# Nine modulation pieces moved from the state-space groups into the first group's projections of a hybrid diffusion layer

## The chip, the cores and the metric

The kernel runs on one core of one Trainium2 chip. The metric is device time in microseconds (us): the median over runs of the whole kernel. TensorE (PE) multiplies, with its weight loads shown apart (PEld); VectorE (DVE), ScalarE (ACT) and GpSimd (POOL) do the element-wise work; SyncE (SP) issues nearly all of the transfers.

## The reference, cut to what matters

One layer of a diffusion backbone over 512 latent tokens and 256 context tokens, model width 1024, in float32:

```
mod = silu(c) @ w_mod + b_mod                      # six vectors of 1024: sh1 sc1 gt1 sh2 sc2 gt2
h_lat, h_ctx = modulated RMSNorm of x and of ctx   # needs sh1, sc1 only
p = h @ w_in                                       # z | x, B, C | dt | q k v | gates
x, B, C = silu(conv3(p[x, B, C]))                  # three taps along the tokens
y = bidirectional chunked state-space scan of (x, B, C, dt), 4 groups of 8 heads, 4 chunks of 128 tokens
a = windowed attention with rotary embedding, context keys and a sink
out = (g_ssd * (norm(y*silu(z)) @ w_o_ssd) + g_att * (a @ w_o_att)) @ w_out
x = x + gt1 * out;  x = x + gt2 * convffn(modulate(x, sh2, sc2));  final RMSNorm
```

The last four of the six modulation vectors (gt1, sh2, sc2, gt2: 4 x 1024 numbers) are what the moved pieces work on. They are first used after the state-space part.

## The kernel before

Every float32 product is made of three reduced-precision products: a weight tile `wraw` is rounded to `whi` on ScalarE (line 149), the rest `wlo` is formed on VectorE (line 150), and TensorE multiplies `whi` with the high and low part of the activations and `wlo` with the high part (lines 197, 198 and 200 in `gemm`). A weight tile is 128 x 1024 float32, 512 KB.

**Loads.** `load_raw` (line 145) issues a tile's transfer on SP's queue into one of three `wraw` buffers. `whi` and `wlo` have two buffers each. `run(prog)` walks a list of steps, each with the weight tiles that it needs; before a step's instructions are recorded, the loads up to one tile beyond that step are recorded, in the order of the list. A buffer is taken again when the last reader of its old tile is done: for a projection's tile that is the split on lines 149 and 150, for a modulation tile the second operation of its piece.

**The stretch around the change.** After the attention comes the state-space part (its list is built at lines 1523 to 1545). `proj_steps(g)` gives six projections for group g. In this document those of the first group are called b (B), c (C) and x0 to x3. Each multiplies a tile with the latent tokens (24 matmuls of 512 columns) and, except c, with the context tokens (24 of 256 columns). `conv_silu` then makes the convolution: one ScalarE operation (line 1267), two on VectorE (1268, 1269), a tanh on ScalarE (1275) and a last VectorE operation (1276), for the latent tokens and then for the context. The result is transposed on TensorE within the next projection (line 1295) and copied out by ScalarE. `ssd_steps(g)` then does the scan of group g, chunk by chunk, woven with a `z` projection and the projections of group g+1. After x3 the first of these, called z15 here, is a gate projection with the latent tokens alone.

**The modulation pieces.** `m_step(i)` (line 569) is a piece of the product of silu(c) with the modulation matrix. It needs one 512 KB tile `wm2`, which goes through the same three `wraw` buffers but is not split: two VectorE operations on 128 x 512 multiply its halves with two columns of `csil` and add to `tm`, of which there is one buffer (lines 581 and 583). Four pieces make one column group; after the fourth, four transposes on TensorE (line 591) and two short VectorE operations (lines 593, 594) put the sums into `mod2`. There are 32 pieces. Pieces 0 to 8 (m0 to m8 here) lie in the state-space groups 0 to 2, three in each; the others come later.

**What sets the order.** The steps' list sets the order in which the code records instructions, and a scheduler then orders each engine's instructions and assigns the buffers. `tc.issue_after(i)` keeps the operations recorded within it from standing ahead of instruction i.

Of the kernel before, what the change touches and what calls it, by code (L numbers as in the profile page):

```python
# [1 line left out]

# [1 line left out]

# [9 lines left out]
ALU = mybir.AluOpType  # L14
# [30 lines left out]
def tile_hybrid_layer(  # L45
# [33 lines left out]
    V, S, G, T = nc.vector, nc.scalar, nc.gpsimd, nc.tensor  # L79
# [28 lines left out]
    def accb():  # L108
        return bank("acc")

    def misb():
        return bank("mis")
# [3 lines left out]
    def tmp(tag):  # L116
        return tpool.tile([P, 512], F32, tag=tag, name=tag, bufs=TMP[tag])
# [73 lines left out]
    def gemm(targets, w, nk=KT, m=P, k0=0, first=True, last=True, ks=None):  # L191
        hi, lo = w
        for k in range(nk) if ks is None else ks:
            wh, wl = hi[:, k * m : (k + 1) * m], lo[:, k * m : (k + 1) * m]
            a, b = first and k == 0, last and k == nk - 1
            for ps, xh, xl in targets:
                T.matmul(ps, wh, xh[:, k0 + k, :], start=a, stop=False)  # L197
                T.matmul(ps, wh, xl[:, k0 + k, :], start=False, stop=False)  # L198
            for ps, xh, xl in targets:
                T.matmul(ps, wl, xh[:, k0 + k, :], start=False, stop=b)  # L200
            if BETWEEN and k % 3 == 1:
                BETWEEN.pop(0)()
# [12 lines left out]
    csil = cpool.tile([P, KT, 2], F32, name="csil")  # L215
# [88 lines left out]
    with tc.tile_pool(name="spool", bufs=1) as sp:  # L304
# [131 lines left out]
        r, W, H = {}, {}, {}  # L436
# [50 lines left out]
        rows = {}  # L487
# [47 lines left out]
        for i in range(NG):  # L535
            t = tmp("tb")
# [33 lines left out]
    def m_step(i):  # L570
        cg, kk = i // 4, i % 4

        def fn(r):
            if kk == 0:
                macc[0] = tmp("tm")
            acc = macc[0]
            for u in range(2):
                k = 2 * kk + u
                sc = csil[:, k, 0:1]
                if k == 0:  # L580
                    V.tensor_scalar_mul(acc, r[:, 0:512], sc)
                else:
                    V.scalar_tensor_tensor(acc, r[:, u * 512 : u * 512 + 512], sc, acc, ALU.mult, ALU.add)
            if kk == 3 and cg > 5:
                ps = misb()
                T.matmul(ps, ones, acc, start=True, stop=True)
                V.tensor_tensor(F["g2"][cg - 6], ps, F["g2"][cg - 6], ALU.add)
            elif kk == 3:
                ps = misb()
                for c in range(4):  # L590
                    T.transpose(ps[:, c * P : (c + 1) * P], acc[:, c * P : (c + 1) * P], ident)
                z = slice(4 * cg, 4 * cg + 4)
                V.tensor_reduce(mod2[:, z], ps.rearrange("p (c q) -> p c q", c=4), axis=AX.X, op=ALU.add)
                V.tensor_tensor(mod2[:, z], mod2[:, z], vec[:, V_BMOD + 16 + 4 * cg : V_BMOD + 20 + 4 * cg], ALU.add)

        return [("m", i)], fn
# [68 lines left out]
    Q, F = {}, {}  # L665
# [600 lines left out]
    def conv_half(ps, n, base_w, base_b, i, stride, o):  # L1266
        S.activation(o[:, :n], ps[:, :n], AF.Identity, scale=hcol(base_w, stride + i), bias=hcol(base_b, i))  # L1267
        V.scalar_tensor_tensor(o[:, 1:n], ps[:, 0 : n - 1], hcol(base_w, i), o[:, 1:n], ALU.mult, ALU.add)  # L1268
        V.scalar_tensor_tensor(o[:, 0 : n - 1], ps[:, 1:n], hcol(base_w, 2 * stride + i), o[:, 0 : n - 1], ALU.mult, ALU.add)  # L1269

    def conv_silu(ps, n, i, o):
        a = tmp("ta")
        conv_half(ps, n, V_CW, V_CB, i, 24, a)
        t = tmp("tb")
        F["conv"] = S.activation(t[:, :n], a[:, :n], AF.Tanh)  # L1275
        V.scalar_tensor_tensor(o[:, :n], t[:, :n], 1.0, a[:, :n], ALU.add, ALU.mult)

    def flat(a):
        return a.rearrange("p a b -> p (a b)")
# [10 lines left out]
    def turn(n=None):  # L1290

        for t, n_, put in TURN[:n]:
            ps = misb()
            for c in range(n_):
                T.transpose(ps[:, c * P : (c + 1) * P], t[:, c * P : (c + 1) * P], ident)
            put(ps)
        del TURN[:n]

    def proj_steps(g):
        d = GR[g]  # L1300

        def b_fn(w):
            d["xs"] = bp.tile([P, 4, 512], F32, tag="xs", name="xs", bufs=2)
            d["xsc"] = bp.tile([P, 2, 512], F32, tag="xsc", name="xsc", bufs=1)
            d["Bkc"] = bp.tile([P, 2, P], F32, tag="Bkc", name="Bkc", bufs=2)
            d["Bk"] = bp.tile([P, 4, P], F32, tag="Bk", name="Bk", bufs=2)
            d["BT"] = bp.tile([P, L], F32, tag="BT", name="BT", bufs=2)
            pl, pc = accb(), accb()
            gemm([LAT(pl)], w)
            turn()  # L1310
            gemm([CTX(pc)], w)
            conv_silu(pl, L, 16 + g, d["BT"])
            BTc = tmp("tc")
            conv_silu(pc, LC, 16 + g, BTc)
            for t, n, k in ((d["BT"], 4, d["Bk"]), (BTc, 2, d["Bkc"])):
                TURN.append((t, n, lambda ps, n=n, k=k: S.copy(flat(k), ps[:, : n * P])))

        def c_fn(w):
            d["CT"] = bp.tile([P, L], F32, tag="CT", name="CT", bufs=2)
            pl = accb()  # L1320
            gemm([LAT(pl)], w)
            turn()
            conv_silu(pl, L, 20 + g, d["CT"])

        def x_fn(ct, w):
            i = 4 * g + ct
            pl, pc = accb(), accb()
            gemm([LAT(pl)], w)
            turn()
            gemm([CTX(pc)], w)  # L1330
            for pp, n, dst in ((pl, L, d["xs"]), (pc, LC, d["xsc"])):
                xl = tmp("tc")
                conv_silu(pp, n, i, xl)
                TURN.append(
                    (
                        xl,
                        n // P,
                        lambda ps, n=n, dst=dst: S.copy(
                            dst[:, :, ct * P : (ct + 1) * P], ps[:, :n].rearrange("p (a b) -> p a b", b=P)
                        ),  # L1340
                    )
                )

        r = [([("x", 16 + g)], b_fn), ([("x", 20 + g)], c_fn)]
        for ct in range(4):
            r.append(([("x", 4 * g + ct)], lambda w, ct=ct: x_fn(ct, w)))
        return r
# [173 lines left out]
        return r + [([], gate)]  # L1521

    msteps = [m_step(i) for i in range(32)]
    prog = proj_steps(0)
    for g in range(4):
        s = ssd_steps(g)
        f = fill[n2 + g : n2 + 1 + g]
        b = proj_steps(g + 1) if g < 3 else fill[n2 + 4 : n3]
        m = msteps[3 * g : 3 * g + 3] if g < 3 else []

        prog += s[0:1] + f + b[0:1] + s[1:2] + m[0:1] + b[1:2]
        for c in range(4):
            prog += s[3 * c + 2 : 3 * c + 3] + (s[3 * c + 4 : 3 * c + 5] if c < 3 else [])
            if g == 3 and c:
                prog += s[3 * c : 3 * c + 1]
            prog += b[2 + c : 3 + c]
            if c == 1:
                prog += b[6:]
            if g < 3 or c == 3:
                prog += s[3 * c + 3 : 3 * c + 4]  # L1540
            if c in (1, 2):
                prog += m[c : c + 1]
        prog += s[13:14]
    run(prog)
    bpool.close()
# [616 lines left out]
```

## Time and profile before

| | |
|---|---|
| median of 3 runs | 1232.01 us (1231.84 to 1232.99) |
| profiled execution: its time | 1232.22 us |
| profiled execution: its span | 1230.4 us |
| what lies outside the span | 1.8 us |
| modulation tiles: time to landing, median of 32 | 4.1 us |

The span runs from the first to the last instruction of one profiled execution; the views give times from its start. The first group's projections stand at 368 to 418 us. A row of the timeline has the start, the duration, the engine and line, the operation with its output and inputs, and in brackets how long the engine was idle before it and what ended that.

### The profile page before, as it was taken

Reading aid. Unit: us, or ns where it says so; the run is one execution under the profiler, and the core shown is the slowest. Engines: PE = TensorE matmul, PEld = TensorE weight load, DVE = VectorE, ACT = ScalarE, POOL = GpSimd, SP = SyncE. Lnnn points to the kernel's source line nnn. Section 1 sums busy time; section 2 is a strip of 40 time slices with the busy share of each in tenths; the row PEclk is TensorE's granted clock in tenths of the full one; section 3 lists DMA queues with packets and bytes.
Section 4 is the critical chain, followed back from the end, with each engine's and each line's share of the span. In section 5 each row is a group of like instructions: output and inputs, shape, how many; then the busy total and the mean of one; then the engine's idle time right before and its main releaser. Section 6 shows DMA issues by size and latency. Waiting matters only on the chain.

```text
span 1230.4 us, 17460 instructions
## 1 busy us (share of the span) xinstructions
PE 1218.5 (99%) x6328; PEld 996.3 (81%) x6328; DVE 914.1 (74%) x1484; ACT 687.0 (56%) x1302; POOL 167.9 (14%) x174
## 2 busy tenths in 40 slices
PE   9999999999999999999999999999999999999997
PEld 6798888888878877777777778888988888888886
DVE  4757888888555698697886786677688788886566
ACT  4657787787443556566586572223544444444543
POOL 0000111121100033333351530000200000000000
PEclk9999999999999999999999999999999999999999
DMA  9652678877946235345347466776144444457785
GB/s 354 245 159 89 218 194 194 212 198 211 225 141 211 91 123 147 121 131 185 122 138 203 136 205 221 225 245 236 48 166 148 145 150 153 153 169 248 243 318 183
DMA packets 108630, 224.65 MB, mean 183 GB/s; under 512 B 9600, under 2 KB 48832, under 8 KB 108544
## 3 DMA queue, kind: packets, MB, share of 16 engines
q1 hardware_dynamic: 101056, 197.32, 48.9%
q0 software_dynamic: 6912, 25.17, 8.7%
q8 instruction: 50, 0.82, 0.3%
q10 hardware_dynamic: 576, 1.05, 0.2%
q14 instruction: 36, 0.29, 0.1%
HBM read 193.29 MB, written 49.87 MB: 198 GB/s over the span
## 4 chain that ended last, share of the span: by engine, by line
PE 92%; DVE 3%; DMA 2%; ACT 2%; issue 1%; SPq 0%; POOLq 0%; ACTq 0%; DVEq 0%
PE acc L197 19%; PE acc L200 19%; PE acc L198 19%; PE acc L1919 3%; PE acc L1917 3%; PE acc L1918 3%; PE score L811 3%; PE po L860 3%; PE pt L847 2%; PE mis L1480 2%; PE mis L1385 2%; DMA wm<-wm 1%; PE mis L422 1%; PE acc L930 1%; PE acc L931 1%; PE acc L932 1%
## 5 line engine op out<-in xcount | busy, mean ns | idle before, releaser
L197 PE MATMUL acc<-hlh,whi 128*128 128x512 f32 x488 | 199.3, 408 | 0.0
L150 DVE TENSOR_TENSOR wlo<-wraw,whi 128x1024 fp32r<-128x1024 f32 (+2 forms) x119 | 143.4, 1207 | 71.9 <-ACT whi L149 62.2
L149 ACT CAST whi<-wraw 128x1024 fp32r<-128x1024 f32 (+2 forms) x119 | 122.8, 1033 | 127.4 <-PE acc L198 75.0
L200 PE MATMUL acc<-hlh,wlo 128*128 128x512 f32 x488 | 191.4, 392 | 0.0
L198 PE MATMUL acc<-hll,whi 128*128 128x512 f32 x488 | 190.7, 391 | 0.0
L197 PE MATMUL acc<-mh,whi 128*128 128x512 f32 x360 | 141.0, 392 | 0.0
L200 PE MATMUL acc<-mh,wlo 128*128 128x512 f32 x360 | 140.1, 389 | 0.0
L198 PE MATMUL acc<-ml,whi 128*128 128x512 f32 x360 | 140.0, 389 | 0.0
L200 PEld LDWEIGHTS acc<-hlh,wlo 128*128 128x128 f32 x488 | 91.6, 188 | 20.3
L198 PEld LDWEIGHTS acc<-hll,whi 128*128 128x128 f32 x488 | 91.9, 188 | 17.5 <-issue 1.7
L197 PEld LDWEIGHTS acc<-hlh,whi 128*128 128x128 f32 x488 | 91.8, 188 | 17.5 <-issue 2.2
L198 PEld LDWEIGHTS acc<-ml,whi 128*128 128x128 f32 x360 | 67.6, 188 | 14.5 <-issue 0.5
L197 PEld LDWEIGHTS acc<-mh,whi 128*128 128x128 f32 x360 | 67.6, 188 | 14.3 <-issue 0.5
L200 PEld LDWEIGHTS acc<-mh,wlo 128*128 128x128 f32 x360 | 67.6, 188 | 14.2
L820 DVE CUSTOM_DVE_ANT_0 p<-score,winm,nsink 128x512 f32<-128x512 f32 (+1 forms) x64 | 51.9, 810 | 15.2 <-PE score L811 13.7
L1268 DVE SCALAR_TENSOR_TENSOR ta<-acc,half,ta 128x511 f32<-128x511 f32 (+1 forms) x66 | 43.8, 663 | 25.7 <-ACT ta L1267 25.6
L1267 ACT ACTIVATE ta<-acc,half 128x512 f32<-128x512 f32 (+1 forms) x66 | 46.7, 708 | 27.0 <-PE acc L200 25.7
L1275 ACT ACTIVATE tb<-ta 128x512 f32<-128x512 f32 (+1 forms) x44 | 23.5, 534 | 65.2 <-DVE ta L1269 59.2
L827 ACT ACTIVATE p<-p,mneg 128x512 f32<-128x512 f32 (+1 forms) x64 | 49.7, 777 | 15.3 <-DVE mneg L820 14.7
L1387 POOL TENSOR_TENSOR st<-st,eT 128x512 f32<-128x512 f32 x24 | 33.5, 1396 | 170.5 <-ACT st L1405 162.3
L197 PE MATMUL acc<-hch,whi 128*128 128x256 f32 x176 | 54.4, 309 | 0.0
L855 DVE TENSOR_TENSOR ptl<-pt,pth 128x512 fp32r<-128x512 f32 x72 | 47.5, 686 | 8.5 <-ACT pth L851 7.8
(503 smaller groups left out, 2970.1 us busy)
## 6 DMA issues: line engine op xcount, KB each, us to landing
wraw<-wup SPq DMA_DIRECT2D x44, 512.0 KB, 3.6
wt_d<-wdn POOLq DMA_DIRECT2D x36, 512.0 KB, 7.8
fb<-cs_d SPq DMA_DIRECT2D x32, 512.0 KB, 6.6
wraw<-wm SPq DMA_DIRECT2D x32, 512.0 KB, 4.1
wraw<-wx SPq DMA_DIRECT2D x24, 512.0 KB, 3.5
wraw<-wt_d SPq DMA_DIRECT2D x20, 512.0 KB, 4.0
sp_d<-te SPq DMA_DIRECT2D x33, 256.0 KB, 2.1
wm<-wm SPq DMA_DIRECT2D x16, 512.0 KB, 7.7
```

Of the source, the lines that this page charges most:

```text
L149: S.copy(hi[:, :n], r[:, :n])
L150: V.tensor_tensor(lo[:, :n], r[:, :n], raw(hi[:, :n]), ALU.subtract)
L197: T.matmul(ps, wh, xh[:, k0 + k, :], start=a, stop=False)
L198: T.matmul(ps, wh, xl[:, k0 + k, :], start=False, stop=False)
L200: T.matmul(ps, wl, xh[:, k0 + k, :], start=False, stop=b)
L811: T.matmul(ps[:, o : o + len(z) * P], Q[h][:, b * P : (b + 1) * P], k[:, j, z[0] * P : (z[-1] + 1) * P], start=v == 0 and o % 512 in (0, P ...
L820: V.tensor_tensor_reduce(p[:, :w], d["ps"][i][:, o0 : o0 + w], m, op0=ALU.add, op1=ALU.min, scale=1.0, scalar=nsink[:, h : h + 1], accum_o ...
L827: S.activation(p, p, AF.Exp, bias=d["mneg"][:, i : i + 1], scale=-1.0, accum_out=d["den"][:, i : i + 1])
L855: V.tensor_tensor(d["ptl"][x], d["pt"][x], raw(d["pth"][x]), ALU.subtract)
L860: T.matmul(d["po"], vst[:, cols[x], j, :], d[y][x], start=x == 0 and y == "pth", stop=x == c - 1 and y == "ptl")
L1267: S.activation(o[:, :n], ps[:, :n], AF.Identity, scale=hcol(base_w, stride + i), bias=hcol(base_b, i))
L1268: V.scalar_tensor_tensor(o[:, 1:n], ps[:, 0 : n - 1], hcol(base_w, i), o[:, 1:n], ALU.mult, ALU.add)
```

## The change

Pieces m0 to m8 are taken out of groups 0 to 2 and put behind the first group's six projections: one behind b, one behind c, two behind each of x0, x1 and x2, one behind x3. Their VectorE operations are wrapped in `tc.issue_after` on `F["rows"]`, the last VectorE operation of the convolution that was recorded last (the context's; behind c, which has no context, the latent's).

```
-            for u in range(2):
-                k = 2 * kk + u
...
+            with tc.issue_after(F["behind"].ins) if F.get("behind") else nullcontext():
+                for u in range(2):
+                    k = 2 * kk + u
...
-        V.scalar_tensor_tensor(o[:, :n], t[:, :n], 1.0, a[:, :n], ALU.add, ALU.mult)
+        F["rows"] = V.scalar_tensor_tensor(o[:, :n], t[:, :n], 1.0, a[:, :n], ALU.add, ALU.mult)
...
-    prog = proj_steps(0)
+
+    def behind(fn):
+        def late(r):
+            F["behind"] = F["rows"]
+            fn(r)
+            F["behind"] = None
+
+        return late
+
+    prog, m = [], msteps[:9]
+    for step, n in zip(proj_steps(0), (1, 1, 2, 2, 2, 1)):
+        prog += [step] + [(keys, behind(fn)) for keys, fn in m[:n]]
+        m = m[n:]
...
-        m = msteps[3 * g : 3 * g + 3] if g < 3 else []
-
-        prog += s[0:1] + f + b[0:1] + s[1:2] + m[0:1] + b[1:2]
+
+        prog += s[0:1] + f + b[0:1] + s[1:2] + b[1:2]
...
-            if c in (1, 2):
-                prog += m[c : c + 1]
```

From line 577 on, the changed kernel's line numbers are one higher or more. Three places in the order of the instructions are shown, first as it was, then as it is. Tiles have their numbers, so that they can be followed.

SP's transfers around x3 and z15, before: `wraw_4316` is x3's tile, `wraw_4398` z15's, `wraw_4531` that of m0.

```order
L145 DMA wraw_4316<-wx 128x1024
L1433 DMA z_5303<-zs_d_92 128x512 x3
L145 DMA wraw_4398<-wz 128x1024
L1433 DMA z_5303<-zs_d_92 128x512
L145 DMA wraw_4485<-wx 128x1024
L145 DMA wraw_4531<-wm2 128x1024
L145 DMA wraw_4679<-wx 128x1024
L145 DMA wraw_4688<-wx 128x1024
```

The same place now: the `wx` tiles are x1 (`wraw_4243`), x2 (`wraw_4341`) and x3 (`wraw_4431`), the `wm2` tiles are m2 to m8, and `wz` is z15's.

```order
L145 DMA wraw_4171<-wm2 128x1024
L145 DMA wraw_4239<-wm2 128x1024
L1434 DMA z_5343<-zs_d_92 128x512 x4
L145 DMA wraw_4243<-wx 128x1024
L145 DMA wraw_4258<-wm2 128x1024
L145 DMA wraw_4336<-wm2 128x1024
L145 DMA wraw_4341<-wx 128x1024
L145 DMA wraw_4349<-wm2 128x1024
L145 DMA wraw_4427<-wm2 128x1024
L145 DMA wraw_4431<-wx 128x1024
L145 DMA wraw_4446<-wm2 128x1024
L145 DMA wraw_4524<-wz 128x1024
```

Where x3's and z15's tiles were issued one after the other, two modulation tiles now stand ahead of each of x2 and x3. In the built program x1's load takes the buffer of m1 and waits for m1's second operation; x2's takes that of m3, x3's that of m5 and z15's that of m6, and each waits for the second operation of that piece.

VectorE from the end of c's convolution through that of x0, before (`wlo_4237` is the split of x2's tile):

```order
L1276 SCALAR_TENSOR_TENSOR CT_4119<-tb_4159,ta_4155 128x512
L1268 SCALAR_TENSOR_TENSOR ta_4219<-acc_4168,half_86,ta_4219 128x511
L1269 SCALAR_TENSOR_TENSOR ta_4219<-acc_4168,half_86,ta_4219 128x511
L1276 SCALAR_TENSOR_TENSOR tc_4218<-tb_4223,ta_4219 128x512
L1268 SCALAR_TENSOR_TENSOR ta_4227<-acc_4169,half_86,ta_4227 128x255
L1269 SCALAR_TENSOR_TENSOR ta_4227<-acc_4169,half_86,ta_4227 128x255
L150 TENSOR_TENSOR wlo_4237<-wraw_4234,whi_4236 128x1024
L1276 SCALAR_TENSOR_TENSOR tc_4226<-tb_4231,ta_4227 128x256
```

Now (`wlo_4246` is the split of x1's tile; the `tm` rows are m1, m2 and m3):

```order
L1277 SCALAR_TENSOR_TENSOR CT_4120<-tb_4160,ta_4156 128x512
L584 SCALAR_TENSOR_TENSOR tm_4115<-wraw_4118,csil_85,tm_4115 128x512 x2
L1269 SCALAR_TENSOR_TENSOR ta_4224<-acc_4173,half_86,ta_4224 128x511
L1270 SCALAR_TENSOR_TENSOR ta_4224<-acc_4173,half_86,ta_4224 128x511
L150 TENSOR_TENSOR wlo_4246<-wraw_4243,whi_4245 128x1024
L1277 SCALAR_TENSOR_TENSOR tc_4223<-tb_4228,ta_4224 128x512
L1269 SCALAR_TENSOR_TENSOR ta_4232<-acc_4174,half_86,ta_4232 128x255
L1270 SCALAR_TENSOR_TENSOR ta_4232<-acc_4174,half_86,ta_4232 128x255
L1277 SCALAR_TENSOR_TENSOR tc_4231<-tb_4236,ta_4232 128x256
L584 SCALAR_TENSOR_TENSOR tm_4115<-wraw_4171,csil_85,tm_4115 128x512 x2
L584 SCALAR_TENSOR_TENSOR tm_4115<-wraw_4239,csil_85,tm_4115 128x512 x2
```

Between x0's two convolutions the split of the tile after the next stood; now that of the next tile stands there, ahead of the rest of x0's convolution, and m2 and m3 behind that.

TensorE at the start of x1, now (`whi_4245` and `wlo_4246` are x1's tile; before, these rows went on with `wlo` in the third place):

```order
L200 MATMUL acc_4174<-hch_102,wlo_4166 128x256
L197 MATMUL acc_4260<-hlh_100,whi_4245 128x512
L198 MATMUL acc_4260<-hll_101,whi_4245 128x512
L197 MATMUL acc_4261<-hch_102,whi_4245 128x256
L198 MATMUL acc_4261<-hcl_103,whi_4245 128x256
L200 MATMUL acc_4260<-hlh_100,wlo_4246 128x512
```

Two matmuls of x1's context product now stand ahead of the first one that needs `wlo`.

More of the change, by code (lines that the diff above doesn't have):

```diff
@@ L1 @@
-from contextlib import ExitStack
+from contextlib import ExitStack, nullcontext
 import numpy as np
@@ L576, in fn @@
             acc = macc[0]
-            for u in range(2):
-                k = 2 * kk + u
[L579 to L583, printed above, removed]
+            with tc.issue_after(F["behind"].ins) if F.get("behind") else nullcontext():
+                for u in range(2):
+                    k = 2 * kk + u
+                    sc = csil[:, k, 0:1]
+                    if k == 0:
+                        V.tensor_scalar_mul(acc, r[:, 0:512], sc)
+                    else:
+                        V.scalar_tensor_tensor(acc, r[:, u * 512 : u * 512 + 512], sc, acc, ALU.mult, ALU.add)
             if kk == 3 and cg > 5:
```

## Prediction

> **What bounds the kernel now.** I read the page first: the busy times and the chain that ended last.
>
> ```profile
> PE 1218.5 (99%) x6328; PEld 996.3 (81%) x6328; DVE 914.1 (74%) x1484; ACT 687.0 (56%) x1302; POOL 167.9 (14%) x174
> PE 92%; DVE 3%; DMA 2%; ACT 2%; issue 1%; SPq 0%; POOLq 0%; ACTq 0%; DVEq 0%
> ```
>
> TensorE is busy for 99% of the span and carries 92% of the chain. The change takes no matmul away: the transposes of the pieces only move. So it can gain no more than TensorE waits today in the stretch that it touches, and any wait that it brings there is lost in full. TensorE's waits from 360 to 745 us, the first group's projections and the four groups (total, times, longest):
>
> ```profile
> PE mis L1486 <- DVE E L1471: 0.9, 1, 0.9
> PE mis L1385 <- DVE z L1506: 0.5, 1, 0.5
> PE mis L1480 <- ACT xs L1338: 0.3, 1, 0.3
> ```
>
> 1.7 us in all. Next the busy times by stretch (length; PE, PEld, DVE, ACT, POOL busy with instruction counts; clock, DMA share, GB/s): x0 to x3, then ten microseconds of group 0.
>
> ```profile
> 376.20:382.20 6.00, 6.00 (x31) 4.99 (x31) 3.04 (x5) 2.77 (x5) 0.00 (x0) 1.00 0.96 262
> 382.20:390.60 8.40, 8.40 (x51) 7.45 (x50) 4.92 (x6) 3.51 (x7) 0.00 (x0) 1.00 0.82 285
> 390.60:399.60 9.00, 9.00 (x56) 7.99 (x55) 4.75 (x8) 4.38 (x8) 0.00 (x0) 1.00 0.18 60
> 399.60:408.60 9.00, 9.00 (x56) 7.99 (x55) 5.66 (x9) 3.72 (x7) 0.00 (x0) 1.00 0.27 81
> 440.00:450.00 10.00, 10.00 (x55) 7.12 (x54) 10.00 (x18) 2.90 (x5) 1.84 (x3) 1.00 0.41 138
> ```
>
> In the projections VectorE is half idle and, from 390 on, so are the transfers; in group 0 VectorE has no gap. By busy share the pieces fit better into the projections. But a step there is short. The first matmul of x1, x2, x3 and z15:
>
> ```profile
> 390.61 0.40 PE L197 MATMUL acc<-hlh,whi 128*128 128x512 f32 x1
> 399.61 0.40 PE L197 MATMUL acc<-hlh,whi 128*128 128x512 f32 x1
> 408.60 0.40 PE L197 MATMUL acc<-hlh,whi 128*128 128x512 f32 x1
> 417.59 0.40 PE L197 MATMUL acc<-hlh,whi 128*128 128x512 f32 x1
> ```
>
> A step takes 9.0 us, and each must find its tile loaded and split.
>
> **What it removes.** Nine pieces, 18 VectorE operations, leave the groups, and with them a wait of VectorE for a modulation tile:
>
> ```profile
> 480.23 1.37 DVE L583 SCALAR_TENSOR_TENSOR tm<-wraw,csil,tm 128x512 f32<-128x512 f32 x1 [0.90 <-DMA wraw<-wm]
> ```
>
> What that is worth on TensorE is bounded by the three waits above: 0 to 1.7 us. I take 1.2, the waits for `E` and for `xs`; the one for `z` I leave standing, since group 2 has its own VectorE work there. The transposes cost the same at either place:
>
> ```profile
> L591 PE MATMUL mis<-ident,tm 128*128 128x128 f32 x24 | 3.6, 272 | 0.0
> ```
>
> 3.6 us for 24 is 0.6 for a group of four; they overlap in the array, so I count 0.45 of TensorE's time in the projections for each of the two groups, given back later.
>
> **What it adds: a chain of loads.** x1 to x3 and z15 now load into buffers that pieces must first leave. So there is a new chain: a piece's two operations, the load, the cast, the split, and behind the split, on VectorE, the rest of the convolution and the next pieces. Its links, as the trace has them. c's convolution on ScalarE and VectorE, first and last operation, and the end of c's matmuls, at which the transposes start:
>
> ```profile
> 381.63 0.60 PE L1295 MATMUL mis<-ident,BT 128*128 128x128 f32 x4
> 383.29 0.80 ACT L1267 ACTIVATE ta<-acc,half 128x512 f32<-128x512 f32 x1
> 386.41 0.69 DVE L1276 SCALAR_TENSOR_TENSOR CT<-tb,ta 128x512 f32<-128x512 f32 x1 [0.76 <-ACT tb L1275]
> ```
>
> The piece's operations (the first one of a column group, one other, and two others in a row), and the load ahead of the first:
>
> ```profile
> 402.02 0.33 SPq L145 DMA_DIRECT2D wraw<-wm  x1
> 405.53 0.49 DVE L581 TENSOR_SCALAR tm<-wraw,csil 128x512 f32<-128x512 f32 x1 [1.65 <-DMA wraw<-wm]
> 406.05 0.75 DVE L583 SCALAR_TENSOR_TENSOR tm<-wraw,csil,tm 128x512 f32<-128x512 f32 x1
> 794.04 1.53 DVE L583 SCALAR_TENSOR_TENSOR tm<-wraw,csil,tm 128x512 f32<-128x512 f32 x2
> ```
>
> A piece is 1.53 us, or 1.27 (405.53 to 406.80) if it starts a column group; a load on idle transfer engines takes 3.5 us (402.02 to 405.53). Cast, split, and the context's convolution behind the split:
>
> ```profile
> 399.69 1.05 ACT L149 CAST whi<-wraw 128x1024 fp32r<-128x1024 f32 x1 [0.33 <-PE acc L198]
> 400.77 1.23 DVE L150 TENSOR_TENSOR wlo<-wraw,whi 128x1024 fp32r<-128x1024 f32 x1 [0.69 <-ACT whi L149]
> 401.91 0.47 DVE L1268 SCALAR_TENSOR_TENSOR ta<-acc,half,ta 128x255 f32<-128x255 f32 x1
> 403.45 0.43 DVE L1276 SCALAR_TENSOR_TENSOR tc<-tb,ta 128x256 f32<-128x256 f32 x1 [0.55 <-ACT tb L1275]
> ```
>
> Cast and split are 2.31 us (399.69 to 402.00); the context's convolution on VectorE is 1.97 (401.91 to 403.88). The latent's last operation takes 0.61 ahead of the next:
>
> ```profile
> 391.05 0.69 DVE L1276 SCALAR_TENSOR_TENSOR tc<-tb,ta 128x512 f32<-128x512 f32 x1 [0.76 <-ACT tb L1275]
> 391.66 0.48 DVE L1268 SCALAR_TENSOR_TENSOR ta<-acc,half,ta 128x255 f32<-128x255 f32 x1
> ```
>
> *x1.* Its load waits for m1, and m1 for c's convolution. That takes 3.81 us (383.29 to 387.10). In the new order it stands ahead of the two copies, and x1's cast is gone from ahead of it, so it can start when c's matmuls are done: 381.63 and about 0.2 for the hand-over. It ends at 385.65, m1 at 387.2, and then the load is issued. Other transfers are still under way then; the last of them is issued at 384.35, and the transfer engines empty after 388:
>
> ```profile
> 384.35 0.44 SPq L1433 DMA_DIRECT2D z<-zs_d  x1
> 388.00:389.00 1.00, 1.00 (x11) 1.00 (x10) 0.25 (x1) 0.72 (x1) 0.00 (x0) 1.00 0.64 250
> 389.00:390.00 1.00, 1.00 (x10) 1.00 (x10) 0.96 (x2) 0.00 (x0) 0.00 (x0) 1.00 0.22 82
> ```
>
> Two projection tiles give the ends, one issued at 370.12 among other transfers and one at 393.81 on its own:
>
> ```profile
> DMA to landing us min/median/max: 4.7/4.7/4.7
> DMA to landing us min/median/max: 3.4/3.4/3.4
> ```
>
> I take 4.1, between them, since the queue is nearly empty: landed at 391.3, split at 393.6. TensorE comes to x1 at 390.61 and can do four matmuls without `wlo`, two of the 24 latent and two of the 24 context ones: a twelfth of the 8.4 us of x0, 0.7. So it needs `wlo` at 391.3 and waits **2.3 us**.
>
> *x2.* From the end of x1's split: the latent's last operation 0.61, the context's convolution 1.97, m2 and m3 3.06, load 3.5, cast and split 2.31: 11.45 us to the end of x2's split.
>
> *x3.* From there: 1.97, m4 and m5 2.80 (1.27 and 1.53), load 3.5, cast and split 2.31: 10.6 us.
>
> Together 22.0 us, in which TensorE has two steps, 18.0, and four transposes, 0.45: it waits **3.6 us**. Matmuls and transposes put ahead of the waiting one only shift this between x2 and x3.
>
> *z15.* From x3's split: 0.43 for the convolution's last operation, m6 1.53, load 3.5, cast and split 2.31: 7.8 us, less than the step's 9.0; no wait. b, c and x0 keep their places: x0's load takes the buffer of c's tile and is issued where x2's was, at 370.12, long ahead of its use at 382.2.
>
> Behind the waiting cast ScalarE holds the tanh of the step before, and behind the waiting split VectorE holds that step's convolution: it is in the chain above. Behind SP's waiting loads stand only tiles of later steps. The nine tiles of 512 KB add nothing to the full stretch up to 388: up to there m1, m2 and m3 stand where the tiles of later projections stood.
>
> **The sum.** Against the profiled execution (1232.22 us, of which 1230.4 span; 0.2 above the median of 1232.01): 1232.2 + 2.3 + 3.6 - 1.2 = **1236.9 us**. Bounds: the three landings at 3.4 or at 4.7 each give -0.9 or +3.0. If c's convolution keeps its start at 383.29, x1's wait grows by 1.4; if ScalarE's operation for x2's context holds up x3's cast, by some 0.4 there. Gain 0 to 1.7. So 1232.2 + 5.0 - 1.7 = 1235.5 at the best, 1232.2 + 10.7 = 1242.9 at the worst, which needs all of it at once; I take 1241.5 as the upper end.
>
> The Trainium skill, page "DMA: Bandwidth & Descriptors", section "Anatomy of one DMA — SWDGE (gpsimd) path", fits a transfer as 2.0 us and bytes by 436 GB/s; for 512 KB that is an estimate of 3.2 us, by which the three loads cost 1.5 us less and the sum would be 1235.4. These loads go by SP and the trace has 3.4 at the least, so I keep the trace. Its section "Rules for kernel authors" says to issue a transfer early and wait on it late, which speaks against this change for x1 to x3: their loads are issued a step later than now.
>
> **Rivals.**
>
> *The loads stay hidden (faster).* If x1's tile lands by 389.6 and the chain keeps within TensorE's step, only the gain is left: 1232.2 - 1.2 = 1231.0, or 1230.5 with all three waits gone. For it: VectorE and the transfer engines are half idle. Against it: m1 would have to end 1.7 us earlier than worked out, and 11.45 us would have to shrink to 9.4. It decides at a chain of 9.4 us. Chance 0.12.
>
> *Only x1 waits.* The start costs 2.3, then the chain keeps up, through a better overlap of m2 and m3 with ScalarE's part: 1232.2 + 2.3 - 1.2 = 1233.3. Against it: VectorE runs its queue in order and m2, m3 stand behind the context's convolution. Chance 0.10.
>
> *TensorE's clock falls in the waits.* The granted clock is 1.00 in every stretch above; over the whole execution it is
>
> ```profile
> core 0: 1230.4 us, clock 0.998
> ```
>
> so what the start costs is 0.002 x 1230.4 = 2.5 us. If each of three waits cost as much again: 1236.9 + 7.5 = 1244.4. Against it: at most 2.3 us of waiting in one place, by the sum. The Trainium skill, "TensorE: Matmul & The Clock Gate", section "HAM oscillation — how this bites in real kernels", sets the limit for idle gaps at about 3.4 us; by that rule the clock stays. Chance 0.06.
>
> **How the numbers follow.** The forecast has 0.72, 1236.9 us, its own range 1235.5 to 1241.5. With the case in which only x1 waits the range is 1233.0 to 1241.5; left out are the hidden loads and the clock, 0.18. A measurement of this kernel tells about 0.2%, 2.5 us, from no change. Faster by more than that (under 1229.5) is beyond the 1.7 us of waits: 0.03, for waits that the view does not show. Same: the rest of the hidden loads, 0.09, and most of the case in which only x1 waits, 0.08: 0.17. Slower: 0.80.
>
> **What would show it.** Right: TensorE waits for `whi` or `wlo` (line 149 or 150) at x1, x2 and x3, some 6 us together and none at z15; the loads of x1 to x3 issued within 0.1 us of the end of a piece's second operation; 11 us from one split to the next; the wait for `E` gone in group 1; VectorE under 10.0 of 10 in group 0. Wrong: x1's split done by 391.3; a step of 9.0 to 9.5 us from x1 to x2; waits at z15 or b of the next group; or a granted clock under 1.00 in the projections.

## The result, and the profile after

| | before | after |
|---|---|---|
| median of 6 runs each | 1232.32 us (1231.73 to 1233.97) | 1242.39 us (1240.96 to 1243.81) |
| profiled execution: its time / span | 1232.22 / 1230.4 us | 1242.52 / 1240.7 us |

The changed kernel is slower: the ratio is 1.008, with a 95% interval of 1.007 to 1.0091. Forecast were 1236.9 us, 1233.0 to 1241.5: the direction was right, the size was not.

**Where the 10.3 us are.** Five places that both programs pass on TensorE cut the span into stretches: the first matmul of b, the first chunk sums of groups 0 and 3 (line 1403, in the changed kernel 1404), the down projection's first product and its last one. Their rows in the timeline of the kernel before, with those of groups 1 and 2 for later use:

```profile
367.82 0.39 PE L197 MATMUL acc<-hlh,whi 128*128 128x512 f32 x1
...
427.23 1.88 PE L1403 MATMUL mis<-xw,Bkc 128*128 128x512 f32 x4
...
507.25 1.02 PE L1403 MATMUL mis<-xw,Bkc 128*128 128x512 f32 x2
...
588.54 1.88 PE L1403 MATMUL mis<-xw,Bkc 128*128 128x512 f32 x4
...
668.82 1.88 PE L1403 MATMUL mis<-xw,Bkc 128*128 128x512 f32 x4
...
1113.74 0.39 PE L1917 MATMUL acc<-ww,fyh 128*128 128x512 f32 x1
...
1222.03 0.39 PE L1919 MATMUL acc<-ww,ring 128*128 128x512 f32 x1
```

and in that of the changed kernel:

```profile
367.42 0.40 PE L197 MATMUL acc<-hlh,whi 128*128 128x512 f32 x1
...
437.12 1.88 PE L1404 MATMUL mis<-xw,Bkc 128*128 128x512 f32 x4
...
516.25 1.88 PE L1404 MATMUL mis<-xw,Bkc 128*128 128x512 f32 x4
...
595.37 1.88 PE L1404 MATMUL mis<-xw,Bkc 128*128 128x512 f32 x4
...
674.65 1.88 PE L1404 MATMUL mis<-xw,Bkc 128*128 128x512 f32 x4
...
1122.25 0.47 PE L1927 MATMUL acc<-ww,fyh 128*128 128x512 f32 x1 [2.53 <-DVE tc L1821]
...
1232.29 0.39 PE L1929 MATMUL acc<-ww,ring 128*128 128x512 f32 x1
```

| stretch | before | after | difference | forecast |
|---|---|---|---|---|
| start to b | 367.82 | 367.42 | -0.40 | 0 |
| projections: b to group 0 | 59.41 | 69.70 | +10.29 | +6.8 (waits 5.9, transposes 0.9) |
| groups 0 to 2 | 241.59 | 237.53 | -4.06 | -2.1 (waits 1.2, transposes 0.9) |
| group 3 to the down projection | 444.92 | 447.60 | +2.68 | 0 |
| down projection | 108.29 | 110.04 | +1.75 | 0 |

With 0.04 behind the last matmul that is the 10.3 us between the spans. Three terms are off: the projections lose 3.5 us more than worked out, the groups give back twice as much, and 4.4 us are lost where the change touches nothing. The waits of TensorE from 360 to 700 us, after (total, times, longest):

```profile
PE acc L197 <- ACT whi L149: 4.3, 2, 2.4
PE mis L1296 <- DVE tc L1277: 0.6, 1, 0.6
PE acc L200 <- DVE wlo L150: 0.2, 1, 0.2
```

The waits for `E`, `xs` and `z` of before are gone. In their place stand waits at x1 and x3 (4.3 us), a short one for x2's `wlo` (0.2 us), and one for a convolution that has to be transposed (0.6 us). The chain of loads, in rows picked from the timeline (m1; load, cast and split of x1; m2 and m3; load, cast and split of x2; the last operations of m4 and m5; load, cast and split of x3):

```profile
385.15 1.53 DVE L584 SCALAR_TENSOR_TENSOR tm<-wraw,csil,tm 128x512 f32<-128x512 f32 x2
386.71 0.33 SPq L145 DMA_DIRECT2D wraw<-wx  x1
391.67 1.04 ACT L149 CAST whi<-wraw 128x1024 fp32r<-128x1024 f32 x1 [3.33 <-DMA wraw<-wx]
392.74 1.23 DVE L150 TENSOR_TENSOR wlo<-wraw,whi 128x1024 fp32r<-128x1024 f32 x1 [2.84 <-ACT whi L149]
...
396.37 3.11 DVE L584 SCALAR_TENSOR_TENSOR tm<-wraw,csil,tm 128x512 f32<-128x512 f32 x4
399.50 0.33 SPq L145 DMA_DIRECT2D wraw<-wx  x1
403.67 1.05 ACT L149 CAST whi<-wraw 128x1024 fp32r<-128x1024 f32 x1
404.75 1.23 DVE L150 TENSOR_TENSOR wlo<-wraw,whi 128x1024 fp32r<-128x1024 f32 x1 [0.28 <-ACT whi L149]
...
408.29 2.33 DVE L584 SCALAR_TENSOR_TENSOR tm<-wraw,csil,tm 128x512 f32<-128x512 f32 x3
410.65 0.33 SPq L145 DMA_DIRECT2D wraw<-wx  x1
414.97 1.04 ACT L149 CAST whi<-wraw 128x1024 fp32r<-128x1024 f32 x1
416.05 1.23 DVE L150 TENSOR_TENSOR wlo<-wraw,whi 128x1024 fp32r<-128x1024 f32 x1
```

Each load is issued within 0.03 us of the end of the pieces ahead of it (385.15 + 1.53 = 386.68; 396.37 + 3.11 = 399.48; 408.29 + 2.33 = 410.62), as the forecast has it. From issue to cast it takes 4.96, 4.17 and 4.32 us, where 4.1, 3.5 and 3.5 were put in; the loads themselves land after 4.9, 4.1 and 4.3 us. The clock, by stretch (columns as before; PEclk is the third number from the end):

```profile
392.00:396.00 4.00, 3.24 (x9) 2.68 (x10) 2.70 (x4) 2.11 (x4) 0.00 (x0) 0.57 0.18 46
416.00:420.00 4.00, 3.93 (x11) 3.11 (x12) 3.89 (x7) 0.43 (x2) 0.00 (x0) 0.57 0.39 113
450.00:460.00 10.00, 10.00 (x55) 7.13 (x54) 10.00 (x20) 4.07 (x9) 2.74 (x3) 1.00 0.29 107
1124.00:1128.00 4.00, 4.00 (x14) 3.21 (x13) 4.00 (x8) 2.35 (x5) 0.00 (x0) 0.71 0.80 270
```

Within the work it falls in three places, right behind TensorE's waits at x1 (2.38 us), at x3 (1.88 us) and at the down projection (2.53 us), each time to half for some 3.4 us; the stretches shown are longer than that. The third row is the stretch of group 0 that stands ten microseconds earlier in the kernel before: VectorE is as full there as it was.

**The down projection.** Its first product now waits for line 1821, an operation of the last up projection. It uses nothing of that operation's result. But its accumulator is the first tile of a new pool over all eight PSUM banks, and that is bank 0 in both programs. The tile that the last up projection's convolution reads lies in bank 1 before and in bank 0 after. The five banks of `mis` are handed on in the order of their release, and the transposes of m3 and m7, which take one each, now come earlier in that order. So the new wait would be for the bank. That is a reading of the two built programs; the first two experiments test the wait, and the handing on they leave as read.

### The profile page after: what moved, and what is told of

Same layout as the page of the kernel before. It is cut to its first block, busy times and chain, and to the rows that moved or that the text cites. A ratio compares the mean times of both kernels' runs of the same rounds, so it can differ in the third digit from the quotient of the medians.

```text
span 1240.7 us, 17465 instructions
## 1 busy us (share of the span) xinstructions
PE 1223.0 (99%) x6328; PEld 1000.3 (81%) x6328; DVE 912.5 (74%) x1484; ACT 687.1 (55%) x1302; POOL 165.8 (13%) x174
## 4 chain that ended last, share of the span: by engine, by line
PE 91%; DMA 3%; DVE 3%; ACT 1%; issue 1%; POOL 0%; SPq 0%; POOLq 0%; ACTq 0%; DVEq 0%
PE acc L197 19%; PE acc L200 19%; PE acc L198 19%; PE score L812 3%; PE po L861 3%; PE pt L848 2%; PE mis L1481 2%; PE acc L1927 2%; PE acc L1929 2%; PE acc L1928 2%; PE mis L1386 2%; PE mis L1487 1%; DMA wm<-wm 1%; PE acc L931 1%; PE mis L422 1%; PE acc L932 1%
```

## The experiments

The theory: three separate things make the difference. (1) The held pieces keep the weight buffers, so that x1 to x3 load late. (2) Idle time of about 2 us makes TensorE's clock fall, and what then runs slowly is partly on the path. (3) A shifted rotation of PSUM banks puts a wait into the down projection. Rivals: VectorE's work itself makes the splits late; the clock falls for another reason; VectorE is simply late at the end.

**The bank, taken away and put in.** One edit serves for both kernels: the down projection's first tile gets bank 1, its second bank 0.

```
-            m, f_ = [accb(), accb()], [accb()]
+            m, f_ = [accb(), bank("one")], [accb()]
...
-        psum_pools(acc=(8, 1))
+        psum_pools(one=(1, 1), acc=(7, 1))
```

On the changed kernel:

> The changed kernel with one edit at its end: the down projection's first product takes PSUM bank 1 for its first token tile and bank 0 for its second, where before both came from a pool of eight that gives bank 0 to the first. Theory 'bank': TensorE's wait of 2.53 us ahead of that product is for bank 0, which the last up projection held, and the clock falls behind it, 4.4 us together. With bank 1 the first half product (2.0 us) runs while VectorE empties bank 0, so about 0.5 us of wait is left and no drop of the clock: 3.9 us less, about 1238.5. Rival 'late VectorE': VectorE is late there for another reason, and the product waits whatever its bank: no change, 1242.4. Rival 'clock by its own': the wait goes but the clock still falls there: about 1240.5.

On the kernel before:

> The kernel before with the same edit of the down projection's banks. There the last up projection held bank 1, so the edit makes the first product wait for VectorE where it did not. Theory 'bank': a wait of about 2.5 us and a clock that falls behind it, 1.7 us: 1232.3 + 4.2 = 1236.5. Rival 'late VectorE': the bank is of no account, 1232.3.

Measured: 1238.88 us for the first (ratio to the kernel before 1.0059, 1.0046 to 1.0071), 3.5 us under the changed kernel, which was timed at another time (in the two traces it is 3.05 us from group 3 to the last matmul); 1235.62 us for the second (1.0025, 1.0014 to 1.0035), 3.7 us over the kernel before, whose runs beside them gave 1231.94. The wait that is left in the first, at the second half of the product (total, times, longest):

```profile
PE one L1927 <- DVE tc L1821: 1.2, 1, 1.2
```

And the second, whose end now reads as that of the changed kernel did:

```profile
1115.43 0.75 PE L1917 MATMUL acc<-ww,fyh 128*128 128x512 f32 x1 [2.53 <-DVE tc L1811]
...
1225.45 0.39 PE L1919 MATMUL acc<-ww,ring 128*128 128x512 f32 x1
```

The same wait of 2.53 us comes with the bank alone, and with the other bank it goes. From the first product to the last matmul it is 110.02 us here, as in the changed kernel, and 108.29 without the wait; from group 3 to the first product it is 447.58 us, and 444.92 without. That is 2.7 us and 1.7 us. The half product covered less than expected (1.2 us left, not 0.5).

**Does the wait make the clock fall?** The second of these kernels, with matmuls in the wait, into a bank that is free:

```
+            for _ in range(10):
+                T.matmul(m[1], w0[0][:, :P], w0[0][:, 512:], start=True, stop=True, skip_group_check=True)
             product("p1", m, True, True)
```

> The kernel before with the banks that make its down projection wait, and ten matmuls of 128 x 512 (0.23 us from one to the next, 2.3 us) into a bank that is free, ahead of the waiting product: TensorE works through the wait of 2.53 us. Theory 'clock': idle time of 1.9 us and more makes the granted clock fall to half for 3.4 us; without it the clock stays at 1.00 there and from the product's first matmul to the last of the kernel it takes 108.3 us, as in the kernel before, in place of 110.0; the time is 1235.6 - 1.7 = 1233.9. Rival 'new product, not the wait': the clock falls there all the same, 1235.6.

Measured: 1234.43 us (1.002, 1.0011 to 1.0029). Its end:

```profile
1115.70 0.47 PE L1917 MATMUL acc<-ww,fyh 128*128 128x512 f32 x1 [0.27 <-DVE tc L1811]
...
1224.08 0.39 PE L1919 MATMUL acc<-ww,ring 128*128 128x512 f32 x1
```

The product starts as late as before, and yet the rest takes 108.38 us and not 110.02: 1.64 us come back, and up to the last matmul no stretch there is under a clock of 1.00. So it is the idle time that lowers the clock, not the new product. The medians, 1235.62 and 1234.43, differ by less, since the unfilled kernel doesn't lose the clock each time: three of its eight executions have a mean clock of 0.998 and take 1233.9 to 1234.3 us, the other five have 0.996 or 0.997 and take 1235.6 to 1236.2. The eleven of the filled kernel take 1234.0 to 1235.0. The two kernels were timed at different times, and the intervals of their ratios overlap; the traces decide here.

**The clock in the projections.** On the kernel with the banks, matmuls ahead of x3's projection, into the bank that it then begins anew:

```
             pl, pc = accb(), accb()
+            for _ in range(FILL.get(i, 0)):
+                T.matmul(pl, LAT(pl)[1][:, 0, :P], LAT(pl)[1][:, 0, :], start=True, stop=True)
...
+    FILL = {3: 5}
```

> As the run with the banks, and five matmuls of 128 x 512 (0.34 us each, 1.7 us, into the bank that the projection then begins anew) ahead of x3's projection, where TensorE waits 1.9 us for x3's split. Theory 'clock': the wait of 1.9 us is what makes the granted clock fall to about half for 3.4 us; with TensorE busy it stays at 1.00 from 416 to 424, and the kernel is 1.7 us faster than the run with the banks, about 1236.8. Rival 'the start of work, not the wait': the clock falls there all the same, no change or up to 0.3 us slower.

and with `FILL = {1: 9, 3: 5}`:

> The run with the banks, with nine such matmuls ahead of x1's projection (2.1 us) and five ahead of x3's (1.2 us), so that the clock stays at 1.00 in all the projections. Theory 'chain': from x1's split to x3's the pieces and the loads set the time, so a drop of the clock at x1 costs nothing and only that at x3 does, 1.2 us of its 1.7: within 0.4 of the run that fills x3 alone, 1238.0 to 1238.7. Rival 'clock': each drop costs 1.7 us on the path: 1236.8 or below.

Measured: 1238.33 us (1.0049, 1.0037 to 1.0062) and 1238.40 us (1.0049, 1.0037 to 1.0062), beside 1238.88 without filling. Five matmuls take 1.2 us and not the 1.7 of the first expectation, for 0.23 us pass from one to the next. x3 without filling (first matmul, first one with `wlo`, and the first of z15):

```profile
415.50 0.50 PE L197 MATMUL acc<-hlh,whi 128*128 128x512 f32 x1 [2.34 <-ACT whi L149]
...
416.76 0.80 PE L200 MATMUL acc<-hlh,wlo 128*128 128x512 f32 x1
...
426.86 0.40 PE L197 MATMUL acc<-hlh,whi 128*128 128x512 f32 x1
```

and with it:

```profile
415.82 0.49 PE L197 MATMUL acc<-hlh,whi 128*128 128x512 f32 x1 [0.97 <-ACT whi L149]
...
417.09 0.50 PE L200 MATMUL acc<-hlh,wlo 128*128 128x512 f32 x1 [0.30 <-DVE wlo L150]
...
425.97 0.40 PE L197 MATMUL acc<-hlh,whi 128*128 128x512 f32 x1
```

From the first matmul with `wlo` to z15 it is 10.10 us with the slow clock and 8.88 with the full one: 1.2 of the 1.7 us are on the path, the rest passes while x3 waits for `wlo` anyway. From b to group 0 it is 69.73 us without filling and 69.06 with it, 0.67 us of the 1.2, since x3's split came 0.54 us later behind b in the filled run. The medians differ by 0.55 us, with intervals that overlap. The second kernel keeps the clock up at x1 too; over its span it is

```profile
core 0: 1236.3 us, clock 0.999
```

and from b to group 0 it takes 69.13 us, as the first does (69.06). So a drop at x1 costs nothing: the chain of loads sets when x2 and x3 begin. The expectation "chain" holds, the rival "each drop 1.7 us" falls.

**The buffers.** The kernel with the banks, the nine pieces' tiles loaded into four buffers of the tag `fb`, which the scan uses only later:

```
+        if key[0] == "m" and key[1] < 9:
+            r = F["bp"].tile([P, 8, P], F32, tag="fb", name="mw", bufs=4).rearrange("p a b -> p (a b)")
+        else:
             r = wpool.tile([P, 1024], F32, tag="raw", name="wraw", bufs=3)
...
+    F["bp"] = bp
```

> As the run with the banks, and the nine moved pieces load their tiles into the four buffers of another tag of the state-space part, which stand empty during these projections, so that the projections' tiles have the three weight buffers to themselves again. Nothing else moves. Theory 'loads': the waits at x1 to x3 and both drops of the clock go, the stretch from b to z15 takes 49.8 + 0.9 for the transposes = 50.7 us in place of 59.9, and the time is 1238.5 - 9.2 = 1229.3. Rival 'VectorE': the pieces' two operations ahead of each split keep VectorE too busy, and half or more of the waits stay: 1234 or above.

Measured: 1230.28 us, 0.9986 (0.9977 to 0.9995) of the kernel before. TensorE's waits from 360 to 440 us are one row, for the transposes of a piece:

```profile
PE mis L595 <- DVE tm L587: 0.2, 1, 0.2
```

All pieces stand where the change put them, and every wait for a split is gone. The stretch from b to group 0 is 60.91 us: 1.5 over the kernel before in place of 10.3, and 0.9 of it are the transposes. VectorE, with the same work, is no hindrance.

**The hold.** The kernel with the banks, the weight buffers shared again, and no `issue_after`:

```
-            F["behind"] = F["rows"]
+            F["behind"] = None
```

> The run with the banks, without the hold: the pieces' operations are not kept behind the convolution's last operation, so the scheduler puts those of m0 to m3 ahead of the first convolutions. Theory 'loads': it is the hold that keeps the buffers; the tiles of x1 to x3 are issued a step earlier, the waits there and the drops of the clock go, and the time is that with the pieces' own buffers, about 1230.3, within 1.5. Rival 'share of buffers': nine more tiles through three buffers make the projections' loads late whether held or not: 1235 or above.

Measured: 1230.55 us, 0.9988 (0.9979 to 0.9997). The loads of x1 and x3 in its timeline:

```profile
374.01 0.33 SPq L145 DMA_DIRECT2D wraw<-wx  x1
...
397.99 0.33 SPq L145 DMA_DIRECT2D wraw<-wx  x1
```

They go out 12.7 us earlier than in the changed kernel (386.71 and 410.65), through the same three buffers, and no projection waits for its split; from b to group 0 it is 61.47 us, with one wait of 0.8 us for a convolution to be transposed. So it isn't the number of tiles in the buffers, it is that each piece holds its buffer until a convolution is done.

**Fewer pieces.** One piece behind each projection, one in each group, with the hold and the banks:

```
-    for step, n in zip(proj_steps(0), (1, 1, 2, 2, 2, 1)):
+    for step, n in zip(proj_steps(0), (1, 1, 1, 1, 1, 1)):
...
-        prog += s[0:1] + f + b[0:1] + s[1:2] + b[1:2]
+        prog += s[0:1] + f + b[0:1] + s[1:2] + m[g : g + 1] * (g < 3) + b[1:2]
```

> The run with the banks, but one piece behind each of the six projections (m0 to m5), and one in each of groups 0 to 2 (m6 to m8). Theory 'loads': x1's load waits for m1 as before (wait of 1.6 to 2.4 us, with or without a drop of the clock); from x1's split to x2's the chain is 0.61 + 1.97 + 1.53 + 3.5 + 2.31 = 9.9 us against TensorE's 9.0, so some 0.9 us each at x2 and x3, too short for the clock: a loss of 4 to 5 us in place of 8.6; the groups give back two thirds of 4.1; the tail has no wait. 1230.3 - 1.2 + 4.5 + 1.4 = 1235. Rival 'VectorE': it has 1.5 us more to spare in each step, so only x1 waits: 1232 to 1233.

Measured: 1235.73 us (1.0027, 1.0016 to 1.0037), as expected, but not for the reason given. There is no wait at x1. TensorE waits within its queue, for what it has to transpose (lines 1296 and 592):

```profile
397.68 0.44 PE L1296 MATMUL mis<-ident,tc 128*128 128x128 f32 x2 [1.46 <-DVE tc L1277]
...
408.76 0.66 PE L592 MATMUL mis<-ident,tm 128*128 128x128 f32 x4 [2.19 <-DVE tm L584]
```

The second is for m3, whose operations are held behind a convolution while its transposes stand in TensorE's queue. The clock falls behind it:

```profile
408.00:412.00 4.00, 3.24 (x20) 3.24 (x21) 2.84 (x5) 1.17 (x3) 0.00 (x0) 0.74 0.42 155
```

From b to group 0 it is 65.41 us, 6.0 over the kernel before. The groups give back 2.1, nearly all of it in groups 0 and 2. The program gives each group a piece, but the scheduler takes them ahead: in the trace m6 is done before group 0 begins at 432.77, m7 lies in group 0, and m8 in group 1, which ends at 593.01 (a column group's first operation is on line 582):

```profile
563.20 1.47 DVE L582 TENSOR_SCALAR tm<-wraw,csil 128x512 f32<-128x512 f32 x1 [0.43 <-DMA wraw<-wm]
565.78 1.84 DVE L584 SCALAR_TENSOR_TENSOR tm<-wraw,csil,tm 128x512 f32<-128x512 f32 x1
```

Group 2 has no piece there.

**What the pieces cost the groups.** The kernel before, the first eight pieces left out; their sums in `mod2` are set to zero, so this program doesn't compute the layer:

```
+        def fn0():
+            if kk == 3:
+                V.memset(mod2[:, 4 * cg : 4 * cg + 4], 0.0)
...
+        if i < 8:
+            return [], fn0
```

> The kernel before without the first eight pieces m0 to m7: their tiles aren't loaded, their sixteen VectorE operations and eight transposes left out, their mod2 columns are zero; m8 stays in group 2. It shows what the pieces cost the state-space groups by themselves. In the trace of the kernel before, the stretch of the three groups from z15 at 417.59 to the same place of group 3 at 668.82 takes 251.23 us, and 247.33 us in the changed kernel. Theory 'groups': TensorE's stalls there are twice what its idle rows show, 3.2 us beside 0.9 for the transposes; without the pieces the stretch takes 247.2 us and the kernel 1232.0 - 4.1 = 1227.9. Rival, the forecast's sum: only the idle time of 1.2 us and the 0.9 go: 249.1 us, 1229.9. Rival 'elsewhere': the groups gain for another reason than the pieces' leaving: less than 1 us.

Measured: 1229.51 us, 0.9983 (0.9974 to 0.9992). Groups 0 to 2 take 239.15 us, 2.4 less than in the kernel before: in the total the rival's 2.1 is nearer than the theory's 4.1. By group:

| | group 0 | group 1 | group 2 |
|---|---|---|---|
| before | 80.02 | 81.29 | 80.28 |
| after | 79.13 | 79.12 | 79.28 |
| without m0 to m7 | 79.17 | 79.12 | 80.85 |
| one piece in each in the program (the run above) | 79.12 | 81.12 | 79.26 |

A group in which no stall is seen takes 79.12 us. Groups 0 and 1 fall to that when the pieces leave, as in the changed kernel: 3.0 us together, of which 0.45 are transposes. Group 2 gets longer. m8, which stays, runs there at 610.01, where it ran at 644.09 in the kernel before, and TensorE then waits (total, times, longest):

```profile
PE mis L1493 <- DVE E L1478: 1.3, 2, 0.9
```

So the theory "groups" holds for the two groups that the edit empties, and its total of 4.1 isn't reached; that m8's new place is the reason is read from the order of these rows and wasn't tested. What a piece costs depends on where it stands: m8 alone goes with 1.7 us in group 2 here, while m7 in group 0 of the run above goes with none.

**A version that beats both.** Own buffers for the pieces, and the last up projection's bank given to the fourth tile of the down projection:

```
-            m, f_ = [accb(), bank("one")], [accb()]
+            m, f_ = [accb(), accb()], [accb()]
...
-            f_.append(accb())
+            f_.append(bank("one"))
```

> The run with own buffers for the pieces' tiles, and the bank that the last up projection held given to the fourth tile of the down projection in place of the second. Theory 'bank': the 1.2 us that the first product's second half still waited go: 1230.3 - 1.2 = 1229.1, which is 0.24% under the kernel before. Rival: the wait moves on to the next thing that is late there, 1230.3.

Measured: 1229.66 us, 0.9982 (0.9973 to 0.9991) of the kernel before, 2.1 us less. The interval overlaps that of the run with own buffers alone (0.9977 to 0.9995), so the second edit's share isn't shown by the medians. In the trace the down projection is at 108.29 us again, as the theory has it, but 0.6 of the 1.4 us are lost at 819 us, at a split that is late in this execution and wasn't in the one with the other bank (total, times, longest):

```profile
PE acc L203 <- DVE wlo L153: 0.3, 1, 0.3
```

Whether the other bank has to do with that is open; the place lies 290 us ahead of the edit.

## Why the prediction was right in its direction and wrong in its size

The step that took the time out of the range is that the sum put nothing on places where no instruction moves. There 4.4 us were lost; without them the time would be 1238.0 us, inside the range. The other steps, in the order of the prediction:

- **TensorE is the bound, and the gain is limited by its waits.** Right in kind, wrong as a bound. The groups gave back 4.06 us where 1.2 + 0.9 were worked out: the waits of 1.7 us all went, and more. Matmul by matmul beside the changed kernel, the three waits cost 0.43, 1.07 and 0.59 us, where their rows in the view have 0.27, 0.91 and 0.52; about 1.0 us more lies at matmuls with no idle time before them in the view, or less than 0.1. With no stall seen the same matmuls need 79.12 us a group and not 80.0 to 81.3.
- **The chain of loads.** Right in its links: m1's end, the load behind it, no wait at z15, and the two kernels without the hold or with own buffers show that nothing else makes a projection wait for its tile. Mis-sized were the loads: 4.96, 4.17 and 4.32 us to the cast, for 4.1, 3.5 and 3.5. x3's split ended 49.86 us behind b (416.05 + 1.23 - 367.42) where the forecast had 47.78, 2.1 us more. The trace has a piece's tile under way when x2's load is issued; that it is this that slows the load is argued only.
- **The clock in the waits** was a rival with a chance of 0.06, and it came true, at a smaller price than the 2.5 us for each wait that it was given: nothing at x1, 1.2 us at x3. That price was itself a misreading. The mean clock of 0.998 was put down to the start, but in the trace of the kernel before the clock is 1.00 there and falls at the end, behind the last matmul, where it costs nothing:

```profile
0.00:4.00 4.00, 2.90 (x13) 2.90 (x14) 0.69 (x4) 1.50 (x2) 1.11 (x10) 1.00 0.35 90
1226.00:1230.40 4.40, 0.00 (x0) 0.00 (x0) 0.38 (x1) 0.35 (x1) 0.00 (x0) 0.50 0.32 119
```

The step that failed is the reason against it, "by that rule the clock stays". The Trainium skill, "TensorE: Matmul & The Clock Gate", section "HAM oscillation — how this bites in real kernels", sets the limit for idle gaps at about 3.4 us; here waits of 1.88 to 2.53 us were enough, and the measurement decides.

- **The sum took no cost where no instruction moves.** This is the largest failure: 4.4 us, where 5.5 were missing in all. The prediction looked at the order on each engine and not at which PSUM bank the pools hand out; the bank alone brought 2.7 us of wait and, through the clock, 1.7 more.
- The errors add up: 4.4 for the tail, 2.1 for the loads, 1.1 to 1.2 for the clock at x3 and 0.3 that the rows don't place, less 2.0 that the groups gave beyond the forecast and 0.4 by which b began earlier: 5.5 us, the distance from 1236.9 to 1242.4. Errors of 2.4 us pointed the other way, so it is partly luck that the forecast came as near as it did. The worst case of 1242.9 us reached far enough, but out of other terms than these.
- Of what would show it: the waits at x1 and x3, the loads at the end of the pieces, 12.0 and 11.3 us from split to split, no wait at z15 and the missing wait for `E` were seen. The waits for the splits are 4.5 us, not some 6. Not seen: more than 0.2 us of waiting for x2's split, where the slow clock had used up the time, and VectorE under 10.0 of 10 in group 0. It is full there still; its fullness was no measure of what it held up. A granted clock under 1.00 in the projections had been named as what would show the forecast wrong, and it did.

## What to carry to other kernels

A buffer that is held until a late operation delays whatever loads into it next; before pieces go into idle time, ask when they let go of their buffers, and give them buffers of another stage that stand empty then. When instructions move, look where pools that hand out banks in turn come out at the next change of pools: a shift by one there can put in a wait far away, here some 700 us behind the last piece that was moved. And price a wait of 2 us on TensorE at up to 1.7 us more, unless the chain behind it waits anyway; whether it comes can differ from one execution to the next.

## What the runs showed of the hardware

In the profiled executions the granted clock fell to half for 3.41 us behind every wait of TensorE of 1.88 us and more (1.88, 2.19, 2.34, 2.37, 2.38, and 2.53 twice), and behind none of 0.97, 1.17, 1.18, 1.46 and 1.64 us. Where nothing else waited this cost 1.6 to 1.75 us: 110.02 and 110.04 us against 108.38 with the wait filled and 108.29 without it. Filling the wait with matmuls that nobody reads kept the clock at 1.00. These waits are counted from the modelled end of the matmul before, so the true gap may be a little longer.

The traces show more than a length. The drops start on a fixed raster: in the changed kernel at 392.45, 416.35 and 1122.91 us, which are 7 and 207 steps of 3.413 us apart, and in every trace with more than one drop they are whole numbers of such steps apart. In the step right ahead of each drop TensorE was idle for 1.88 us or more (of the 2.38 us at x1 2.07 fell into it); the most in a step with no drop behind it was 1.64 us. So about half a step of idle time was the limit here, and a wait that straddles two steps need not reach it. That would explain why three of eight executions kept the clock in spite of the bank's wait; none of those was traced, so it is argued only.

The same stretches came out alike in the profiled executions to about a tenth of a microsecond: groups 0 to 2 took 237.41 to 237.54 us in all seven profiled kernels with the nine pieces outside them, and 241.59 to 241.62 in the three with them inside. A difference of 0.1% of the whole can be read there from one profiled execution.
